# An encoder layer with neighbourhood attention on one Trainium2 core: TensorE in a written order, scores directly behind the keys, the values' projection among the score steps

## The chip, the cores and the metric

The kernel runs on one core of one Trainium2 chip. The metric is the device time of one execution in microseconds (us). The kernel before takes 1509.41 us (median of 3 runs, 1507.68 to 1510.08).

## The reference

One layer of an encoder on 1024 real tokens behind 16 meta tokens, model width 1024, float32. An RMSNorm, one combined input projection, a branch of neighbourhood attention (8 heads of width 64) and a branch with a gated linear recurrence, both gated and joined, an output projection, and a feed-forward part. The change lies in the attention branch and in the projections of its queries, keys and values:

```python
a = rms_norm(h, norm_mix[l])
(q_na, k_na, v_na, ...) = split_cols(a @ w_in[l])
...
def neighbourhood_attention(q, k, v, rpb):
    # a real token sees an 8 x 16 window of the 64-wide grid, and all 16 meta keys
    s_win = einsum('brchd,bjrwhd->...', qg, k_blk) * dh ** -0.5
    s_win = where(in_win, s_win + bias, -1e30)
    s = concatenate([s_win, s_meta], axis=-1)
    p = softmax(s, axis=-1)
    o_grid = einsum(p_win, v_blk) + einsum(p_meta, vm)
```

## The kernel before, in words

Matrix products are made in three passes with operands that are split into a high and a low part (`mm3`, L122 to L124: high times high, high times low, low times high). The weights come in blocks of 128 columns: `load_block` loads a block over SP's queue (`raw`, L102), ScalarE writes its high part `hi` (L112, or L115 with a factor for the queries), VectorE its low part `lo` (L113 or L116). Each of `raw`, `hi` and `lo` has two buffers. The block after next therefore gets its `hi` and `lo` only when the projection that used the same buffer has ended. `proj_steps` starts that split (`early[nxt]`) at the start of a projection.

The attention works on four pairs of heads (`for p in range(NPAIR)`). For each pair it projects the queries (`ev_q`), the keys (`ev_k`, with the meta keys in `mev_k`) and the values (`ev_vn`). Each projection is three pieces of 24 matmuls for the keys and values (256, 272 and 512 columns) or two pieces for the queries (512 each), into PSUM tiles `mm` out of three banks. The last piece of the keys leaves PSUM like this: ScalarE copies the high part of head 0 and of head 1 into `KS` (L802), VectorE writes the low parts into `KL` (L805), ScalarE copies `KS` onto the other half of the partitions (L807). A strip holds 8 columns of all 16 grid rows, so every strip needs the last piece.

Then come 16 steps, one for each strip `s` of 8 and each head `i` of 2. `scores` makes two matmuls into `nsc` (L848 with `KS`, L849 with `KL`; two banks), VectorE subtracts the mask and finds the extreme (L854), ScalarE takes the exponential (L856), VectorE scales by the reciprocal of the sum (L857, L858). `values` turns the weights (L869, L871: transposes on TensorE into `ppt`, tag "t", two banks), ScalarE and VectorE split them into `PT` (L880, L881), and after every fourth step it makes the products with the values into `pov` (L885 to L894), which leave over `low` (L896, VectorE) and `OT` (L898). The values themselves are turned once a pair (L831 into `vpt`, on the same two banks as `ppt`) and split into `Vn` (L833, L834). At most three steps are open (`pend`).

What sets the order: in the written part (`in_order`, up to the keys of pair 0) the engines run what the code says. After that a scheduler puts each engine's instructions in a row when the program is built. It is the scheduler that moves projections of the next pair, or the first gate products behind pair 3 (L928 to L930), between the score steps. The rows are fixed then: at run time each engine takes its row in order and waits at a semaphore where an operand is not there.

Of the kernel before, what the change touches and what calls it, by code (L numbers as in the profile page):

```python
# [9 lines left out]
F32 = mybir.dt.float32  # L10
# [3 lines left out]
ALU = mybir.AluOpType  # L14
# [4 lines left out]
P = 128  # L19
D = 1024  # L20
KC = D // P
T = 1024
TH = 512
# [3 lines left out]
NPAIR = 4  # L27
# [4 lines left out]
C_QN, C_KN, C_VN, C_Q, C_ZF, C_ZB, C_I, C_G, C_GN, C_GH = (  # L32
    0, 512, 1024, 1536, 2048, 2560, 3072, 3584, 4096, 5120)
# [15 lines left out]
def layer(ctx: ExitStack, tc: tile.TileContext, x, meta, w_in, w_na, w_hg, w_o, w_up, w_dn,  # L49
# [23 lines left out]
    def bank(tag, name):  # L73
        return banks[tag].tile([P, 4, P], F32, tag=tag, name=name)
# [58 lines left out]
    def proj(*args, **kw):  # L133
        for _ in proj_steps(*args, **kw):
            pass
# [15 lines left out]
    def block_of(col):  # L151
        return early.pop(col, None) or load_block(w_in[:, col:col + P], KC, -0.125 if C_QN <= col < C_KN else None)
# [551 lines left out]
    early = {}  # L704
# [27 lines left out]
        next(cur)  # L732
        prev = cur

    def first_query():

        hi, lo = block_of(C_QN)
        early[C_KN] = block_of(C_KN)
        for h in range(2):
            ps = bank("mm", "mm").rearrange("p a b -> p (a b)")  # L740
            for k in range(KC):
                mm3(ps, hi[:, k], lo[:, k], *(t[:, k, :TH] for t in aT[h]), k == 0, k == KC - 1)
            yield ps

    in_order = ExitStack()
    in_order.enter_context(tc.manual_schedule(engines={e.engine for e in (pe, act, dve)}))
    query_ps = list(first_query())
    list(prev)
    hps.close()

# [6 lines left out]
    with (tc.tile_pool(name="npr", bufs=1, side="right", reuse_waits="tile") as npr,  # L757
# [10 lines left out]
        def strips(t, p0, t0, n, w=None):  # L768

            a = t[p0:p0 + 64, 0:8, t0 // 8:(t0 + n) // 8]  # L770
            return a.rearrange("p s (r c) -> p s r c", c=8)

        def grid(ps, p0):
            return ps[p0:p0 + 64].rearrange("p (r s c) -> p s r c", s=8, c=8)

        for p in range(NPAIR):
            NB = npl.tile([P, 2, 1024], F32, tag="NB", name="NB")
            for i in range(2):
# [8 lines left out]
            def ev_q(ps, t0, n):  # L787
                for i in range(2):
                    act.copy(strips(QX[i], 64 * i, t0, n), grid(ps, 64 * i))
                for i in range(2):  # L790
                    b = 64 * i
                    dve.tensor_tensor(strips(QX[i], 64 - b, t0, n), grid(ps, b),
                                      strips(QX[i], b, t0, n).bitcast(F32), op=ALU.subtract)
            if p == 0:
                for h in range(2):
                    ev_q(query_ps[h], h * TH, TH)
            else:
                proj(C_QN + p * P, ev_q)

            def ev_k(ps, t0, n):  # L800
                for i in range(2):
# [7 lines left out]
            def mev_k(ps):  # L809
                for i in range(2):  # L810
# [12 lines left out]

            def mev_vn(ps):
                act.copy(vT[:, 8, P - NM:], ps)
            proj(C_VN + p * P, ev_vn, mev_vn)
            for b in (0, 4, 8):
                pt = bank("t", "vpt")
                m = min(4, 9 - b)
                for j in range(m):  # L830
                    pe.transpose(pt[:, j], vT[:, b + j], ident)  # L831
                src = pt[:, :m].rearrange("p j (i d) -> p j i d", i=2)
                act.copy(V[:, b:b + m, :, :64], src)  # L833
                dve.tensor_tensor(V[:, b:b + m, :, 64:], src, V[:, b:b + m, :, :64].bitcast(F32), op=ALU.subtract)  # L834

            block_sums(p, lambda: npl.tile([P, TH], F32, tag="bs", name="rt", bufs=3))

            po = {}
# [22 lines left out]
            def values(s, i, js, pr):  # L861
# [16 lines left out]
                for k, n, b in runs:  # L878
                    hi = PH[:, b:b + 3 * n - 2:3]
                    act.copy(hi, pt[:, k:k + n])  # L880
                    dve.tensor_tensor(PL[:, b:b + 3 * n - 2:3], pt[:, k:k + n], hi.bitcast(F32), op=ALU.subtract)  # L881
                if e < 3:
                    return
                ov = bank("b", "pov")
                pe.matmul(ov, V[:, 8, i], PH[:, 9:22:4], start=True, stop=False)  # L885
                for a in range(-1, 5):
# [6 lines left out]
                        pe.matmul(ov[:64, e0:e0 + ne], V[:, j, i, :64], PL[:, b:b + ne], start=False, stop=False)  # L893
                pe.matmul(ov, V[:, 8, i], PL[:, 9:22:4], start=False, stop=True)  # L894
                low = npr.tile([64, 4, P], F32, tag="low", name="low")
                dve.tensor_copy(low, ov[64:])  # L896
# [5 lines left out]
            pend = []  # L902
# [880 lines left out]
    with tc.manual_schedule(engines={sp.engine, dve.engine, act.engine, pool.engine}):  # L1783
# [5 lines left out]
        for n, (p_, m) in enumerate(steps):  # L1789
# [101 lines left out]
```

## Time and profile before

| | |
|---|---|
| median of 3 runs | 1509.41 us |
| the profiled execution's own time | 1509.18 us |
| its span in the profile | 1507.4 us |
| TensorE (PE) busy | 1491.1 us, 99% |
| VectorE (DVE) busy | 1045.3 us, 69% |
| ScalarE (ACT) busy | 670.0 us, 44% |
| GpSimd (POOL) busy | 363.2 us, 24% |

The profile gives for each instruction its start and duration on its engine, which tile it writes and reads, and what it waited for. A matmul's duration covers its way through the array, so successive matmuls overlap. The pace of TensorE is read from the distance of two starts. "PEld" is the load of the weights into the array, which runs ahead of the matmul. L12 is line 12 of the kernel.

### The profile page before, as it was taken

To read this page: it belongs to the slowest core of one execution; us is meant where nothing else is said; L and a number is where in the kernel's file an instruction comes from. 1 tells how busy PE (TensorE), PEld (TensorE's weight loads), DVE (VectorE), ACT (ScalarE), POOL (GpSimd) and SP (SyncE) were. 2 spreads that over 40 slices of the span, in tenths; PEclk is the share of its full clock that TensorE was granted. 3 is DMA by queue.
4 is the path that set the end of the run, shared out by engine and by line. 5 is a ranking of instruction groups with operands and counts; after the bars stand their busy time and mean duration, and the time that the engine had idled before them with its cause. 6 is when DMAs were issued, how large, how long until landed. Compare 5 with 4: busy or idle time off the path is not lost.

```text
span 1507.4 us, 23483 instructions
## 1 busy us (share of the span) xinstructions
PE 1491.1 (99%) x9200; PEld 1249.7 (83%) x9200; DVE 1045.3 (69%) x1612; ACT 670.0 (44%) x1197; POOL 363.2 (24%) x346
## 2 busy tenths in 40 slices
PE   9999999999999999999999999999999999999998
PEld 8888888888888888888888887888888888888886
DVE  7777767756786786675475479777777445877876
ACT  7131313135565576334233345555555534334444
POOL 3313131324414400110000121244444200231142
PEclk9999999999999999999999999999999999999999
DMA  4211111114222227444656124444444576563224
GB/s 170 59 29 57 29 56 31 44 31 131 85 65 95 98 85 264 140 148 169 223 160 223 42 96 164 167 154 154 154 154 154 202 255 233 190 229 114 96 84 154
DMA packets 142592, 195.61 MB, mean 130 GB/s; under 512 B 8193, under 2 KB 90369, under 8 KB 142481
## 3 DMA queue, kind: packets, MB, share of 16 engines
q1 hardware_dynamic: 133216, 172.86, 34.8%
q10 hardware_dynamic: 7088, 13.91, 2.4%
q0 software_dynamic: 2176, 7.34, 1.3%
q8 instruction: 72, 1.18, 0.3%
q14 instruction: 40, 0.32, 0.1%
HBM read 139.56 MB, written 54.53 MB: 129 GB/s over the span
## 4 chain that ended last, share of the span: by engine, by line
PE 87%; DVE 6%; DMA 2%; ACT 2%; issue 1%; POOL 1%; SPq 0%; ACTq 0%; POOLq 0%; DVEq 0%
PE mm L122 9%; PE mm L124 9%; PE mm L123 9%; PE mm L1564 5%; PE pa L1564 5%; PE pb L928 4%; PE pb L929 4%; PE pb L930 4%; PE pc L1564 4%; PE pb L1564 4%; PE pc L929 3%; PE pc L930 3%; PE pc L928 3%; PE pa L929 2%; PE pa L930 2%; PE pa L928 2%
## 5 line engine op out<-in xcount | busy, mean ns | idle before, releaser
L122 PE MATMUL mm<-aT,hi 128*128 128x512 f32 (+2 forms) x600 | 215.2, 359 | 0.0
L124 PE MATMUL mm<-aT,lo 128*128 128x512 f32 (+2 forms) x600 | 212.2, 354 | 0.0
L123 PE MATMUL mm<-aT,hi 128*128 128x512 f32 (+2 forms) x600 | 211.6, 353 | 0.0
L97 DVE TENSOR_TENSOR dl<-ur,dh 128x1024 fp32r<-128x1024 f32 x54 | 71.1, 1316 | 87.3 <-ACT dh L96 87.1
L96 ACT CAST dh<-ur 128x1024 fp32r<-128x1024 f32 x54 | 56.9, 1054 | 166.7 <-issue 91.1
L122 PEld LDWEIGHTS mm<-aT,hi 128*128 128x128 f32 x600 | 113.7, 190 | 12.6
L124 PEld LDWEIGHTS mm<-aT,lo 128*128 128x128 f32 x600 | 113.5, 189 | 12.8
L123 PEld LDWEIGHTS mm<-aT,hi 128*128 128x128 f32 x600 | 113.7, 190 | 11.6
L1352 ACT ACTIVATE uv<-uv 128x512 f32<-128x512 f32 x48 | 30.4, 633 | 79.3 <-DVE uv L1460 52.8
L112 ACT CAST hi<-raw 128x1024 fp32r<-128x1024 f32 x26 | 27.3, 1050 | 68.4 <-PE mm L123 65.4
L854 DVE CUSTOM_DVE_ANT_0 pr<-nsc,NB 128x432 f32<-128x432 f32 (+1 forms) x64 | 35.2, 559 | 29.7 <-issue 29.5
L1655 POOL TENSOR_TENSOR w<-w,tt 128x512 f32<-128x512 f32 x16 | 23.4, 1461 | 133.1 <-DVE tt L1654 112.3
L303 POOL TENSOR_TENSOR Y<-X,TN 128x512 f32<-128x512 f32 x20 | 31.6, 1578 | 85.1 <-DVE X L300 85.1
L113 DVE TENSOR_TENSOR lo<-raw,hi 128x1024 fp32r<-128x1024 f32 x26 | 39.5, 1520 | 15.8 <-ACT hi L112 11.8
L124 PE MATMUL mm<-wh,mT 128*128 128x512 f32 x128 | 50.0, 391 | 0.4 <-DVE mT L97 0.4
L122 PE MATMUL mm<-wh,mT 128*128 128x512 f32 x128 | 50.3, 393 | 0.0
L123 PE MATMUL mm<-wl,mT 128*128 128x512 f32 x128 | 50.1, 391 | 0.0
L124 PE MATMUL mm<-o,lo 128*128 128x512 f32 x128 | 49.9, 390 | 0.1
L123 PE MATMUL mm<-o,hi 128*128 128x512 f32 x128 | 49.8, 389 | 0.0
L122 PE MATMUL mm<-o,hi 128*128 128x512 f32 x128 | 49.8, 389 | 0.0
L1564 PE MATMUL mm<-dl,dh 128*128 128x512 f32 x124 | 48.6, 392 | 0.3 <-DVE dl L97 0.2
L1564 PE MATMUL mm<-dh,dl 128*128 128x512 f32 x124 | 48.3, 389 | 0.0
(459 smaller groups left out, 4434.8 us busy)
## 6 DMA issues: line engine op xcount, KB each, us to landing
raw<-in_w_in SPq DMA_DIRECT2D x56, 512.0 KB, 4.0
ur<-usp SPq DMA_DIRECT2D x54, 512.0 KB, 3.5
raw<-in_w_up SPq DMA_DIRECT2D x16, 1024.0 KB, 6.2
usp<-us SPq DMA_DIRECT2D x60, 256.0 KB, 2.3
sg<-gsp SPq DMA_DIRECT2D x16, 512.0 KB, 5.1
w<-in_w_dn SPq DMA_DIRECT2D x16, 512.0 KB, 4.6
usp<-uv SPq DMA_DIRECT2D x30, 256.0 KB, 2.3
gsp<-gv ACTq DMA_DIRECT2D x24, 256.0 KB, 2.4
```

The source lines that it names most:

```text
L96: act.copy(hi, src)
L97: dve.tensor_tensor(lo, src, hi.bitcast(F32), op=ALU.subtract)
L113: dve.tensor_tensor(lo[:, :kc], raw[:, :kc], hi[:, :kc].bitcast(F32), op=ALU.subtract)
L122: pe.matmul(ps, lh, rh, start=first, stop=False)
L123: pe.matmul(ps, lh, rl, start=False, stop=False)
L124: pe.matmul(ps, ll, rh, start=False, stop=last)
L303: pool.tensor_tensor(fap(Y, h, mid3), fap(X, h, mid3), fap(TT, 0, [[4, g], [n + 3, 2], [0, h]]), op=ALU.mult)
L854: dve.tensor_tensor_reduce(out=pr[:, :w], in0=sc[:, :w], in1=NB[:, i, o:o + w], scale=1.0, scalar=3.0e38, op0=ALU.add, op1=ALU.min, accum_ ...
L928: pe.matmul(ps, lhs[0][:, c], rhs[0][:, k], start=first and k == 0, stop=False, skip_group_check=True)
L929: pe.matmul(ps, lhs[0][:, c], rhs[1][:, k], start=False, stop=False, skip_group_check=True)
L930: pe.matmul(ps, lhs[1][:, c], rhs[0][:, k], start=False, stop=k == 3, skip_group_check=True)
L1564: pe.matmul(ps, a[n == 2][:, q, j * P:(j + 1) * P], b[n == 1][:, q], start=first and n == 0, stop=last and n == 2, skip_group_check=True)
```

## The change

The four projections and the 16 steps of each pair stay as they are, number and shape of all matmuls too. What changes is their order, which is now written out for TensorE (`manual_schedule` for `pe.engine`), up to step 6 of pair 3. After that the scheduler orders TensorE again, and VectorE and ScalarE are ordered by it throughout, behind the keys of pair 0.

- The scores of a pair stand directly behind the last piece of its keys.
- The values' projection, the turning of the values and the next pair's queries (`fills`) are the filler between the score steps. A table `GAPS` says how many columns of it go into each step.
- The weights of a step are turned three steps later instead of two (`len(pend) > 3`), and the products stand apart from `values`, one step on.
- The last three turnings of a pair and its last products (`tail`) go between the matmuls of the next pair's keys.
- `low` is copied by ScalarE (`act.copy`, L924) and no longer by VectorE.

```diff
+        def ev_q(h, i):
+            b = 64 * i
+            ps = query_ps[h]
+            act.copy(strips(QX[i], b, h * TH, TH), grid(ps, b))
+            dve.tensor_tensor(strips(QX[i], 64 - b, h * TH, TH), grid(ps, b),
+                              strips(QX[i], b, h * TH, TH).bitcast(F32), op=ALU.subtract)
+
+        def columns(fill, n):
+            ahead_by[0] -= n
+            while ahead_by[0] < 0:
+                ahead_by[0] += next(fill, -ahead_by[0])
+
+        GAPS = ([(830, 830)] * 5 + [(680, 680), (300, 600)]
+                + [(600, 0), (350, 350), (350, 350), (350, 600)] * 2 + [(600, 0)])
...
-            proj(C_KN + p * P, ev_k, mev_k)
+            fill = proj_steps(C_KN + p * P, ev_k, mev_k)
+            for f in tail:
+                columns(fill, 5 * 256)
+                f()
+            list(fill)
             in_order.close()
+            in_order.enter_context(tc.manual_schedule(engines={pe.engine}))
...
-            proj(C_VN + p * P, ev_vn, mev_vn)
-            for b in (0, 4, 8):
...
+            def fills():
+                yield from proj_steps(C_VN + p * P, ev_vn, mev_vn)
+                if p + 1 < NPAIR:
+                    queries = query_steps(p + 1, mm_tile)
+                    for _ in range(2):
+                        yield next(queries)
+                for b in (0, 4, 8):
...
+                if p + 1 < NPAIR:
+                    yield from queries
...
-                dve.tensor_copy(low, ov[64:])
+                act.copy(low, ov[64:])
...
-            for st in steps:
+            fill = fills()
+            pend, due, tail = [], [], []
+            for n, st in enumerate(steps):
                 pend.append((*st, *scores(*st)))
-                if len(pend) > 2:
-                    values(*pend.pop(0))
-            for st in pend:
-                values(*st)
-            pool.dma_start(osp[1][p], OT)
+                if n >= 12 and query_ps and not taken:
+                    ev_q(0, 0)
+                    taken.append((0, 0))
+                if p == NPAIR - 1 and n == 6:
+                    in_order.close()
+                    list(fill)
+                columns(fill, GAPS[n][0])
+                while due:
+                    products(*due.pop())
+                if len(pend) > 3:
+                    s, i, *q = pend.pop(0)
+                    values(s, i, *q)
+                    if s % 4 == 3:
+                        due.append((s, i))
+                columns(fill, GAPS[n][1])
+            list(fill)
```

Three places in the rows of the two built programs matter below. First TensorE at the end of the keys of pair 0 (`mm_4171` is their last piece), in the kernel before; `mm_4209` is the first piece of the values:

```order
L122 MATMUL mm_4171<-aT10_89,hi_3949 128x512
L123 MATMUL mm_4171<-aT11_90,hi_3949 128x512
L124 MATMUL mm_4171<-aT10_89,lo_3950 128x512
L122 MATMUL mm_4209<-aT00_87,hi_4099 128x256
L123 MATMUL mm_4209<-aT01_88,hi_4099 128x256
L124 MATMUL mm_4209<-aT00_87,lo_4100 128x256
```

The same place in the changed kernel, where `mm_4239` is the first piece of the values:

```order
L122 MATMUL mm_4171<-aT10_89,hi_3949 128x512
L123 MATMUL mm_4171<-aT11_90,hi_3949 128x512
L124 MATMUL mm_4171<-aT10_89,lo_3950 128x512
L874 MATMUL nsc_4222<-KS0_4067,QX0_4065 128x288
L875 MATMUL nsc_4222<-KL0_4069,QX0_4065 128x288
L122 MATMUL mm_4239<-aT00_87,hi_4099 128x256
L123 MATMUL mm_4239<-aT01_88,hi_4099 128x256
L124 MATMUL mm_4239<-aT00_87,lo_4100 128x256
```

Between the last keys and the first scores there stood 72 matmuls of the values' projection; now nothing stands there. Pairs 1 to 3 read the same.

Second, VectorE at that place in the kernel before (`lo_4206` is the low part of the next pair's query weights, `pr_4329` the first step's scores):

```order
L116 SCALAR_TENSOR_TENSOR lo_4206<-raw_4203,hi_4205 128x1024
L805 TENSOR_TENSOR KL0_4069<-mm_4171,KS0_4067 64x8x64
L805 TENSOR_TENSOR KL1_4070<-mm_4171,KS1_4068 64x8x64
L854 ISA pr_4329,mn_4330<-nsc_4326,NB_4076 128x288
L854 ISA mn_4330 128x1
```

and in the changed kernel:

```order
L116 SCALAR_TENSOR_TENSOR lo_4236<-raw_4233,hi_4235 128x1024
L813 TENSOR_TENSOR KL0_4069<-mm_4171,KS0_4067 64x8x64
L813 TENSOR_TENSOR KL1_4070<-mm_4171,KS1_4068 64x8x64
L880 ISA pr_4225,mn_4226<-nsc_4222,NB_4076 128x288
L880 ISA mn_4226 128x1
```

Nothing moved here: the split of the next weights still stands ahead of the keys' low part. On ScalarE the high part of the same weights (L115) stands ahead of the copies into `KS`, before and now, and in pair 3 the first gate weights (L96, L97) stand there.

Third, TensorE where the values of pair 0 are turned, in the kernel before (`mm_4706` is the next pair's queries, `vpt` the turned values):

```order
L124 MATMUL mm_4706<-aT00_87,lo_4206 128x512
L831 MATMUL vpt_4291<-ident_77,vT_4071 128x128 x4
L831 MATMUL vpt_4298<-ident_77,vT_4071 128x128 x4
L122 MATMUL mm_4706<-aT00_87,hi_4205 128x512
L848 MATMUL nsc_4385<-KS1_4068,QX1_4066 128x288
```

and in the changed kernel, with `ppt` the turned weights of step 2 (counted from 0):

```order
L895 MATMUL ppt_4404<-ident_77,pr_4296 128x128 x3
L897 MATMUL ppt_4404<-ident_77,pr_4296 128x128
L854 MATMUL vpt_4411<-ident_77,vT_4071 128x128 x4
L854 MATMUL vpt_4418<-ident_77,vT_4071 128x128 x4
L874 MATMUL nsc_4425<-KS1_4068,QX1_4066 128x432
L875 MATMUL nsc_4425<-KL1_4070,QX1_4066 128x432
L854 MATMUL vpt_4436<-ident_77,vT_4071 128x128
L122 MATMUL mm_4397<-aT00_87,hi_4235 128x512
```

The values are now turned behind the weights of step 2, where they were turned ahead of the first weights of the pair. All of these tiles take turns on the two banks of tag "t".

More of the change, by code (lines that the diff above doesn't have):

```diff
@@ L733, in layer, with query_steps @@
         prev = cur
-    def first_query():
-        hi, lo = block_of(C_QN)
-        early[C_KN] = block_of(C_KN)
+    query_ps = []
+    def query_steps(p, tile):
+        hi, lo = block_of(C_QN + p * P)
+        early[C_KN + p * P] = block_of(C_KN + p * P)
         for h in range(2):
-            ps = bank("mm", "mm").rearrange("p a b -> p (a b)")
+            ps = tile()
             for k in range(KC):
                 mm3(ps, hi[:, k], lo[:, k], *(t[:, k, :TH] for t in aT[h]), k == 0, k == KC - 1)
-            yield ps
+                if k == KC - 1:
+                    query_ps.append(ps)
+                yield TH
     in_order = ExitStack()
     in_order.enter_context(tc.manual_schedule(engines={e.engine for e in (pe, act, dve)}))
-    query_ps = list(first_query())
+    list(query_steps(0, lambda: bank("mm", "mm").rearrange("p a b -> p (a b)")))
     list(prev)
@@ L785, in layer @@
                                        op=ALU.subtract)
[L787 to L798, printed above, removed]
             def ev_k(ps, t0, n):
@@ L816, in mev_k @@
                     dve.tensor_tensor(KL[i][b:b + 64, :, P:], m, hi.bitcast(F32), op=ALU.subtract)
-            proj(C_KN + p * P, ev_k, mev_k)
+            for q in ((0, 0), (0, 1), (1, 0), (1, 1)):
+                if q not in taken:
+                    ev_q(*q)
+            query_ps.clear()
+            taken.clear()
+            fill = proj_steps(C_KN + p * P, ev_k, mev_k)
[3 more added lines that the diff above has]
+            list(fill)
             in_order.close()
+            in_order.enter_context(tc.manual_schedule(engines={pe.engine}))
             def ev_vn(ps, t0, n):
@@ L825, in mev_vn @@
                 act.copy(vT[:, 8, P - NM:], ps)
-            proj(C_VN + p * P, ev_vn, mev_vn)
-            for b in (0, 4, 8):
[L828 to L834, printed above, removed]
+            def fills():
[5 more added lines that the diff above has]
+                for b in (0, 4, 8):
+                    pt = bank("t", "vpt")
+                    m = min(4, 9 - b)
+                    for j in range(m):
+                        pe.transpose(pt[:, j], vT[:, b + j], ident)
+                    src = pt[:, :m].rearrange("p j (i d) -> p j i d", i=2)
+                    act.copy(V[:, b:b + m, :, :64], src)
+                    dve.tensor_tensor(V[:, b:b + m, :, 64:], src, V[:, b:b + m, :, :64].bitcast(F32), op=ALU.subtract)
+                    yield m * P // 3
+                if p + 1 < NPAIR:
+                    yield from queries
             block_sums(p, lambda: npl.tile([P, TH], F32, tag="bs", name="rt", bufs=3))
@@ L881, in values, with products @@
                     dve.tensor_tensor(PL[:, b:b + 3 * n - 2:3], pt[:, k:k + n], hi.bitcast(F32), op=ALU.subtract)
-                if e < 3:
-                    return
+            def products(s, i):
+                g = s // 4
+                PH, PL = po[i]
                 ov = bank("b", "pov")
@@ L901, in layer, with last @@
             steps = [(4 * g + e, i) for g in range(2) for i in range(2) for e in range(4)]
-            pend = []
-            for st in steps:
+            fill = fills()
+            pend, due, tail = [], [], []
+            for n, st in enumerate(steps):
                 pend.append((*st, *scores(*st)))
-                if len(pend) > 2:
-                    values(*pend.pop(0))
-            for st in pend:
-                values(*st)
-            pool.dma_start(osp[1][p], OT)
+                if n >= 12 and query_ps and not taken:
[14 more added lines that the diff above has]
+            list(fill)
+            def last(s, i, *q):
+                return lambda: values(s, i, *q)
+            tail += [last(*q) for q in pend]
+            tail += [lambda dst=osp[1][p]: (products(7, 1), pool.dma_start(dst, OT))]
+            if p == NPAIR - 1:
+                for f in tail:
+                    f()
     def winograd(eng, a11, a12, a21, a22, s1, s2, s3, s4):
```

2 lines of the change are left out of this document (added).

## The prediction

> **What bounds the kernel now.** I read the page first, then the stages, then the waits in the attention (330 to 565 us), then single stretches.
>
> ```profile
> span 1507.4 us, 23483 instructions
> PE 1491.1 (99%) x9200; PEld 1249.7 (83%) x9200; DVE 1045.3 (69%) x1612; ACT 670.0 (44%) x1197; POOL 363.2 (24%) x346
> ```
>
> The first row of the table by stage is the attention; its columns are length, then busy time of PE, PEld, DVE, ACT and POOL, and last the granted clock and the DMA's share:
>
> ```profile
> 330.00:565.00 235.00, 233.41 (x1412) 200.51 (x1411) 175.90 (x436) 146.57 (x342) 80.77 (x81) 1.00 0.28 90
> ```
>
> TensorE is busy for 99% of the span, and for 233.41 of the 235.00 us of the attention. It is idle there for 1.6 us by its modelled ends. VectorE has 59 us to spare there, ScalarE 88. So time can only come from TensorE: from waits that go, or from new ones. The number of its matmuls and their shapes stay, so nothing else is to be had.
>
> Who waited for whom in the same stretch (total us, times, longest):
>
> ```profile
> DVE pr L854 <- issue: 29.5, 4, 8.2
> PEld nsc L848 <- DVE mn L854: 5.3, 17, 0.6
> PEld ppt L869 <- issue: 4.0, 14, 0.5
> PEld pov L885 <- ACT PT L880: 1.7, 8, 0.2
> ```
>
> The first row is VectorE standing still four times, up to 8.2 us, while TensorE projects the values of a pair. That is what the new order fills, but VectorE is not the bound. The other three rows are the weight loads of scores, turnings and products, held up by 11.0 us in all. A load runs ahead of its matmul, so most of this passes while TensorE still works; 1.6 us is what shows as its idle time. The waits that the new order can remove are worth between 1.6 and 11.0 us.
>
> **The scores directly behind the keys: a new wait, four times.** The first scores need `KS` and `KL` of the last piece of the keys. What this takes shows at pair 0, where TensorE went on with the values' projection at 348.93:
>
> ```profile
> 348.93 0.28 PE L122 MATMUL mm<-aT,hi 128*128 128x256 f32 x1
> 348.90 1.06 ACT L115 ACTIVATE hi<-raw 128x1024 fp32r<-128x1024 f32 x1 [1.86 <-PE mm L123]
> 349.98 1.19 ACT L802 CAST KS<-mm 64x512 fp32r<-64x512 f32 x2
> 349.99 2.74 DVE L116 SCALAR_TENSOR_TENSOR lo<-raw,hi 128x1024 fp32r<-128x1024 f32 x1 [2.92 <-ACT hi L115]
> 351.07 1.26 ACT L807 CAST KS<-KS 64x512 fp32r<-64x512 f32 x2
> 352.76 1.39 DVE L805 TENSOR_TENSOR KL<-mm,KS 64x512 fp32r<-64x512 f32 x2
> ```
>
> The split of the next weights comes first on both engines, because its buffer falls free with the same last matmul: 1.06 us on ScalarE, then 2.74 us on VectorE. Only then does VectorE write `KL`; the row holds two instructions, so that of head 0 ends after half of 1.39 us, at 353.46. TensorE could have begun the second score matmul then, 4.53 us after the keys. It did not wait, since the values' projection covered this: in pair 1 from 406.31 to 417.67. The same stretch in pairs 1, 2 and 3:
>
> ```profile
> 406.31 0.28 PE L122 MATMUL mm<-aT,hi 128*128 128x256 f32 x1
> 407.38 1.23 DVE L116 SCALAR_TENSOR_TENSOR lo<-raw,hi 128x1024 fp32r<-128x1024 f32 x1 [2.79 <-ACT hi L115]
> 408.64 1.39 DVE L805 TENSOR_TENSOR KL<-mm,KS 64x512 fp32r<-64x512 f32 x2
> 417.67 0.29 PE L848 MATMUL nsc<-KS,QX 128*128 128x288 f32 x1
> ...
> 462.75 0.28 PE L122 MATMUL mm<-aT,hi 128*128 128x256 f32 x1
> 463.81 2.73 DVE L116 SCALAR_TENSOR_TENSOR lo<-raw,hi 128x1024 fp32r<-128x1024 f32 x1 [2.92 <-ACT hi L115]
> 466.57 1.39 DVE L805 TENSOR_TENSOR KL<-mm,KS 64x512 fp32r<-64x512 f32 x2
> ...
> 518.62 0.28 PE L122 MATMUL mm<-aT,hi 128*128 128x256 f32 x1
> 519.68 1.53 DVE L97 TENSOR_TENSOR lo<-raw,hi 128x1024 fp32r<-128x1024 f32 x1 [2.92 <-ACT hi L96]
> 521.24 1.39 DVE L805 TENSOR_TENSOR KL<-mm,KS 64x512 fp32r<-64x512 f32 x2
> ```
>
> By the same reading (start of `KL` plus 0.70, less the end of the keys) these are 3.03, 4.52 and 3.32 us. The rows of the changed program keep the split ahead of `KS` and `KL` in all four pairs, and nothing stands between the keys and the scores on TensorE, so the cover is gone and all of it becomes idle time of TensorE: 4.53 + 3.03 + 4.52 + 3.32 = 15.4 us. Behind the waiting matmul on TensorE stands the whole values' projection, which needs none of this. The ends: the split takes 1.23 us on VectorE at its best and 2.74 at its worst, so four times 3.0 to 4.5 us, 12.0 to 18.0 us. I take 15.4, the sum as it stands.
>
> **The clock behind a wait.** No wait of 3 us occurs in this trace's attention. The nearest row is the one place where the granted clock (next to last but one column) fell, and the stretch around 890 us for comparison:
>
> ```profile
> 59.68:63.09 3.41, 1.81 (x70) 0.99 (x68) 3.41 (x6) 0.37 (x1) 0.08 (x1) 1.00 0.28 83
> 63.09:66.51 3.42, 3.42 (x10) 2.76 (x11) 1.32 (x4) 0.52 (x2) 1.54 (x1) 0.50 0.00 0
> 889.11:892.53 3.42, 2.56 (x15) 1.90 (x14) 2.94 (x5) 2.15 (x5) 0.00 (x0) 1.00 0.02 6
> 892.53:895.94 3.41, 3.41 (x18) 2.88 (x17) 3.27 (x6) 2.86 (x6) 0.00 (x0) 1.00 0.67 200
> ```
>
> After 3.41 us with 1.6 us of idle time the next 3.42 us ran at half the clock; after 3.42 us with 0.86 us of it they did not. A matmul of 512 columns then starts every 0.42 us and no longer every 0.22:
>
> ```profile
> 64.18 0.63 PE L123 MATMUL mm<-aT,hi 128*128 128x512 f32 x1
> 64.60 0.63 PE L124 MATMUL mm<-aT,lo 128*128 128x512 f32 x1
> ...
> 67.09 0.39 PE L122 MATMUL mm<-aT,hi 128*128 128x512 f32 x1
> 67.31 0.39 PE L123 MATMUL mm<-aT,hi 128*128 128x512 f32 x1
> ```
>
> A wait of 3.0 to 4.5 us puts at least 1.5 us of idle time into one such stretch, however it falls. So I expect a slow stretch behind each of the four, worth half of 3.42, 1.7 us, less what of it TensorE still spends waiting, more where the wait reaches into two of them. I take 1.5 us each, 6.0 us. Ends: 0 if the clock holds, 2.9 us each (1.7 us, and half of what a second stretch has left, some 2.3 us) or 11.6 us.
>
> The Trainium skill, "TensorE: Matmul & The Clock Gate", section "Part 1: The HAM clock gate (the "warmup" mystery)", has the gate fall to half rate after an idle window of about 3.4 us that runs freely, and its closing table asks for no idle gaps over about 3 us. That speaks against this change. Read strictly, a whole idle window, it would spare the waits of 3.0 and 3.3 us and hit the two of 4.5 us at most, 3.4 us in place of 6.0 and a sum lower by 2.6 us. The trace fell after less than half a window of idle time and does not agree with the strict reading; I go by the trace.
>
> **Between the score steps.** The groups that matter, by line (busy us and mean ns of one behind the bar):
>
> ```profile
> L881 DVE TENSOR_TENSOR PT<-ppt,PT 128x512 fp32r<-128x512 f32 (+3 forms) x70 | 41.5, 598 | 0.9 <-ACT PT L880 0.3
> L880 ACT CAST PT<-ppt 128x512 fp32r<-128x512 f32 (+3 forms) x71 | 36.2, 514 | 20.8 <-PE ppt L871 18.8 <-DVE PT L881 1.4 <-PE pov L892 0.4
> L896 DVE COPY low<-pov 64x512 f32<-64x512 f32 x15 | 10.4, 692 | 1.7 <-PE pov L894 1.4
> L113 DVE TENSOR_TENSOR lo<-raw,hi 128x1024 fp32r<-128x1024 f32 x7 | 9.9, 1420 | 0.1
> L112 ACT CAST hi<-raw 128x1024 fp32r<-128x1024 f32 x7 | 7.4, 1054 | 13.3 <-PE mm L123 13.2
> ```
>
> Weights that are turned three steps later, with filler in each step, leave the chain of scores, exponential and scaling more time, so the three PEld rows above shrink. I take 4 us off, nearer to the 1.6 of the idle row than to the 11.0, because a PEld wait mostly lies beside running matmuls.
>
> Against it stands the turning of the values, now behind the weights of step 2, on the two banks that `ppt` uses. A bank comes back after a copy on ScalarE (0.51) and a subtraction on VectorE (0.60), 1.1 us, and the split of the next keys' weights (1.05 on ScalarE, then 1.42 on VectorE) starts just then, with the end of the values' projection. Four groups of transposes follow each other with only one pair of scores between them, so TensorE can wait for up to 2.5 us (1.1 and 1.4) in each of pairs 0 to 2, at least not at all. I take 1.0 us, about one bank's return: 3.0 us, from 0 to 7.5.
>
> Edits at nothing: `low` goes from VectorE (0.69 us, 16 times) to ScalarE, which has 88 us free; it would cost some 0.7 us a time only if products had to wait for `pov`, which is used every fourth step. The queries as filler and the tail among the next keys are the same matmuls elsewhere; their copies out of PSUM have a piece of the keys, 3 us or more, ahead of the next use of their bank. SP's and POOL's rows keep their order but for the store of `OT`, which is issued two places later at most and waits for nothing on the path.
>
> **The sum.** The profiled execution took 1509.18 us itself, 1.8 us more than its span and 0.2 under the median, 1509.41. 1509.2 + 15.4 + 6.0 + 3.0 - 4.0 = 1529.6 us.
>
> **The rivals.**
>
> *The clock holds.* The same waits, but no stretch at half rate, and the splits at their shorter durations: between 1509.2 + 12.0 + 3.0 - 4.0 = 1520.2 and 1523.6. For it speaks that the slow stretch in the trace also held small matmuls, which may count for less than a pause between dense ones; against it the two rows with 1.6 and 0.86 us. The skill's strict reading belongs here.
>
> *VectorE falls behind.* The splits are slow in every pair, the waits reach into two stretches, and the turning of the values costs its most: 1509.2 + 18.0 + 11.6 + 7.5 - 4.0 = 1542.3.
>
> *No change.* All 11.0 us of PEld waits were real and go, the four waits are 3.0 us each, the clock holds: 1509.2 - 11.0 + 12.0 = 1510.2.
>
> *Faster.* All 11.0 us go, at steps 4 to 15 of each pair, because VectorE no longer carries a backlog there (the 29.5 us it stood still are used), and the wait behind the keys is only the copy of head 0 and its `KL`, 0.6 + 0.7 = 1.3 us a pair: 1509.2 - 11.0 + 5.2 = 1503.4. It decides in favour of this below a mean wait of 2.75 us a pair. Against it: the split stands ahead of both in the built rows, and the shortest of the four stretches is 3.03 us.
>
> **How the numbers follow.** Forecast (1524 to 1537) 0.55, the clock holds 0.20, VectorE falls behind 0.15, no change 0.06, faster 0.04. The predicted time is that of the first, 1529.6. The range reaches from 1515 to 1540: below it takes in the held clock with a larger gain, above it most of the third case. A measurement here tells 0.2%, 3 us, from no change. Faster 0.04; of "no change" most lies within 3 us, 0.05; slower by over 0.2% is the rest, 0.91.
>
> **What would show it.** In the changed profile: TensorE idle for 3 to 4.5 us right behind each of the four last key pieces, released by `KL` or `KS`; the idle time of VectorE at L854's successor gone; the granted clock at 0.50 for about 3.4 us behind each; waits of `ppt` or `vpt` on VectorE near step 6; fewer PEld waits elsewhere. The prediction is wrong if TensorE's idle time behind the keys is under 2.75 us a pair, if the clock stays at 1.00 there, or if the rest of the steps gains more than 10 us.

## The result and the profile after

The changed kernel takes 1536.73 us (median of 4 runs, 1534.05 to 1537.77) against 1509.63 us (4 runs): a ratio of 1.018, 95% interval 1.0166 to 1.0195. The forecast was 1529.6 us, with a range up to 1540. The direction and the main mechanism came true; the size was 7.1 us short.

The page of the changed kernel, first and third line:

```profile
span 1535.1 us, 23461 instructions
...
PE 1496.8 (98%) x9200; PEld 1256.3 (82%) x9200; DVE 1041.4 (68%) x1596; ACT 682.4 (44%) x1213; POOL 361.7 (24%) x346
```

The same 9200 matmuls are 5.7 us longer busy in a span 27.7 us longer. To see where, I compare the stretch between the 3601st and the 5201st matmul, which holds the attention. First the kernel before, then the changed one (length, then busy time of PE, PEld, DVE, ACT, POOL, then clock and DMA):

```profile
325.49:598.28 272.79, 271.20 (x1602) 232.71 (x1601) 198.48 (x468) 167.83 (x376) 81.79 (x83) 1.00 0.34 111
```

```profile
324.00:626.94 302.94, 278.58 (x1602) 240.76 (x1601) 195.10 (x453) 180.06 (x392) 80.75 (x83) 0.97 0.31 100
```

The stretch grew by 30.15 us. TensorE's idle time in it went from 1.59 to 24.36 us, 22.8 more; its busy time grew by 7.4, at a clock that is no longer 1.00 throughout. (Ahead of the stretch the changed run is 1.5 us better, behind it 1.0: 27.7 in all.) TensorE's waits there, released by whom (total us, times, longest):

```profile
PE nsc L874 <- ACT KS L815: 10.6, 4, 2.6
PE vpt L854 <- DVE PT L907: 4.3, 3, 1.5
PE mm L973 <- ACT go L994: 3.0, 1, 3.0
PE nsc L875 <- DVE KL L813: 2.2, 4, 0.8
PE pov L913 <- ACT PT L906: 2.1, 3, 1.0
PE ppt L895 <- DVE Vn L857: 1.8, 3, 0.6
```

The first and fourth row are the waits behind the keys that the prediction spoke of, 12.8 us by the modelled ends of the matmuls. Counted from start to start, less the pace of a matmul, they are 3.9, 3.9, 3.4 and 3.3 us in the four pairs, 14.5 in all. The other waits are the turning of the values (4.3 and 1.8), the first gate product behind the attention (3.0) and the products (2.1). The keys of pair 0, on all engines; a bracket is the idle time ahead of the instruction and who ended it:

```profile
347.80 0.39 PE L124 MATMUL mm<-aT,lo 128*128 128x512 f32 x1
348.00 1.06 ACT L115 ACTIVATE hi<-raw 128x1024 fp32r<-128x1024 f32 x1 [1.28 <-PE mm L123]
349.08 1.19 ACT L810 CAST KS<-mm 64x512 fp32r<-64x512 f32 x2
349.09 2.12 DVE L116 SCALAR_TENSOR_TENSOR lo<-raw,hi 128x1024 fp32r<-128x1024 f32 x1 [2.34 <-ACT hi L115]
350.17 1.26 ACT L815 CAST KS<-KS 64x512 fp32r<-64x512 f32 x2
350.84 0.40 PE L874 MATMUL nsc<-KS,QX 128*128 128x288 f32 x1 [2.65 <-ACT KS L815]
351.25 1.41 DVE L813 TENSOR_TENSOR KL<-mm,KS 64x512 fp32r<-64x512 f32 x2
352.08 0.37 PE L875 MATMUL nsc<-KL,QX 128*128 128x288 f32 x1 [0.83 <-DVE KL L813]
```

On both engines the split of the next weights (L115, L116) stands ahead of the keys, as the built rows said. The first score starts 3.04 us after the last key matmul, the second another 1.24 later.

Now the clock. The rows are stretches of 3.41 us, cut where the clock may change; the last but two columns are the granted clock and the DMA's share:

```profile
349.53:352.94 3.41, 1.26 (x8) 1.08 (x9) 3.32 (x4) 3.13 (x5) 3.33 (x4) 1.00 0.19 77
352.94:356.36 3.42, 3.42 (x18) 3.42 (x18) 0.38 (x3) 0.63 (x2) 3.01 (x4) 0.50 0.02 5
...
410.97:414.38 3.41, 0.72 (x3) 0.19 (x1) 2.19 (x1) 3.20 (x5) 3.01 (x4) 1.00 0.50 143
414.38:417.79 3.41, 2.62 (x12) 2.62 (x13) 2.43 (x7) 0.78 (x3) 1.83 (x2) 0.50 0.31 85
417.79:421.20 3.41, 3.41 (x16) 3.35 (x16) 0.62 (x2) 0.17 (x1) 0.29 (x1) 0.50 0.66 215
...
479.23:482.64 3.41, 3.16 (x14) 3.16 (x15) 1.89 (x6) 0.78 (x3) 1.29 (x2) 0.50 0.41 92
...
537.26:540.67 3.41, 1.67 (x8) 1.05 (x6) 0.85 (x1) 1.88 (x3) 3.01 (x4) 1.00 0.38 154
540.67:544.08 3.41, 2.29 (x16) 2.08 (x17) 2.65 (x6) 2.09 (x5) 3.10 (x3) 1.00 0.36 98
...
598.70:602.11 3.41, 1.38 (x6) 1.16 (x7) 0.69 (x1) 2.98 (x5) 0.00 (x0) 1.00 1.11 384
602.11:605.52 3.41, 3.41 (x10) 2.64 (x9) 2.32 (x2) 1.96 (x4) 0.00 (x0) 0.50 0.82 317
```

The clock fell behind the keys of pairs 0, 1 (for two stretches) and 2, and behind the wait at the gate products. It did not fall in pair 3, where the same wait lies across the border at 540.67 and leaves 1.67 and 2.29 us of work on either side. Half of the busy time at half clock was lost: (3.42 + 2.62 + 3.41 + 3.16) / 2 = 6.3 us behind the keys, 3.41 / 2 = 1.7 behind the gate products, 8.0 in all.

### The profile page after: what moved, and what is told of

Its sections match the earlier page's. It is cut to its first block, busy times and chain, and to the rows that moved or that the text cites. A ratio compares the mean times of both kernels' runs of the same rounds, so it can differ in the third digit from the quotient of the medians.

```text
span 1535.1 us, 23461 instructions
## 1 busy us (share of the span) xinstructions
PE 1496.8 (98%) x9200; PEld 1256.3 (82%) x9200; DVE 1041.4 (68%) x1596; ACT 682.4 (44%) x1213; POOL 361.7 (24%) x346
## 3 DMA queue, kind: packets, MB, share of 16 engines
q8 instruction: 72, 1.18, 0.3%
## 4 chain that ended last, share of the span: by engine, by line
PE 60%; DVE 2%; ACT 1%; issue 1%; DMA 0%; POOL 0%; SPq 0%; ACTq 0%; POOLq 0%; DVEq 0%
PE mm L1609 5%; PE pa L1609 5%; PE pb L973 4%; PE pb L974 4%; PE pb L975 4%; PE pc L1609 4%; PE mm L124 4%; PE mm L122 4%; PE pb L1609 4%; PE mm L123 4%; PE pc L973 3%; PE pc L975 3%; PE pc L974 3%; PE pa L975 2%; PE pa L973 2%; PE pa L974 2%
## 5 line engine op out<-in xcount | busy, mean ns | idle before, releaser
L122 PE MATMUL mm<-aT,hi 128*128 128x512 f32 (+2 forms) x600 | 219.6, 366 | 0.3 <-DVE QX L784 0.3
L123 PE MATMUL mm<-aT,hi 128*128 128x512 f32 (+2 forms) x600 | 212.5, 354 | 0.0
L96 ACT CAST dh<-ur 128x1024 fp32r<-128x1024 f32 x54 | 56.9, 1054 | 166.7 <-issue 87.7
L97 DVE TENSOR_TENSOR dl<-ur,dh 128x1024 fp32r<-128x1024 f32 x54 | 71.1, 1316 | 87.4 <-ACT dh L96 87.1
L122 PEld LDWEIGHTS mm<-aT,hi 128*128 128x128 f32 x600 | 115.7, 193 | 11.8 <-PE mm L124 0.5
L123 PEld LDWEIGHTS mm<-aT,hi 128*128 128x128 f32 x600 | 115.9, 193 | 10.4
L882 ACT ACTIVATE pr<-pr,mn 128x432 f32<-128x432 f32 (+1 forms) x64 | 40.1, 627 | 43.1 <-DVE mn L880 42.5
L907 DVE TENSOR_TENSOR PT<-ppt,PT 128x512 fp32r<-128x512 f32 (+3 forms) x72 | 42.7, 596 | 8.7 <-ACT PT L906 8.5
```

The costliest lines, as they stand in the source:

```text
L96: act.copy(hi, src)
L97: dve.tensor_tensor(lo, src, hi.bitcast(F32), op=ALU.subtract)
L122: pe.matmul(ps, lh, rh, start=first, stop=False)
L123: pe.matmul(ps, lh, rl, start=False, stop=False)
L882: act.activation(pr[:, :w], pr[:, :w], AF.Exp, bias=mn, scale=-1.0, accum_out=sm)
```

## The experiments

My theory after the result: three things cost time, each a place where TensorE, in its written row, meets work of ScalarE and VectorE that is not ready. They are the keys (14.5 us and 6.3 of half clock), the turning of the values with the products behind it, and the first gate product behind the attention (4.7 us with its half clock). The rivals are in each expectation. The kernels ran in four groups, each against the kernel before on the same chip. The kernel before took 1508.3 to 1509.1 us there, against 1509.63 us beside the changed kernel, which was not run again in them. So what a kernel is said below to gain on the changed kernel by the medians can be too much by 0.5 to 1.4 us:

| kernel | median us | kernel before | ratio, 95% interval |
|---|---|---|---|
| `e1_split_behind` | 1532.34 | 1508.61 | 1.0150 (1.0132 to 1.0168) |
| `e2_values_between` | 1516.38 | 1508.61 | 1.0046 (1.0032 to 1.0060) |
| `e3_dummies` | 1533.24 | 1508.61 | 1.0162 (1.0141 to 1.0182) |
| `e4_turn_bank` | 1531.51 | 1508.61 | 1.0146 (1.0129 to 1.0163) |
| `e5_turn_spread` | 1511.87 | 1508.54 | 1.0022 (1.0012 to 1.0032) |
| `e6_products_later` | 1509.10 | 1508.54 | 1.0006 (0.9996 to 1.0015) |
| `e7_two_open` | 1518.09 | 1508.54 | 1.0062 (1.0046 to 1.0078) |
| `e8_low_back` | 1515.92 | 1508.54 | 1.0051 (1.0033 to 1.0069) |
| `e9_pair3_as_e5` | 1510.31 | 1509.14 | 1.0006 (0.9997 to 1.0015) |
| `e10_one_piece` | 1514.32 | 1509.14 | 1.0039 (1.0024 to 1.0054) |
| `e12_raw_pool` | 1508.32 | 1508.26 | 0.9999 (0.9990 to 1.0008) |
| `e13_after_raw_pool` | 1533.12 | 1508.26 | 1.0165 (1.0152 to 1.0179) |

**The split behind the keys** (`e1_split_behind`). ScalarE and VectorE are put in written order there, too, with the split of the next weights after the keys:

```diff
-            list(fill)
+            for _ in range(23 - kept[0]):
+                next(fill)
+            with tc.manual_schedule(engines={act.engine, dve.engine}) if p else ExitStack():
+                list(fill)
+                if p + 1 < NPAIR:
+                    early[C_QN + (p + 1) * P] = block_of(C_QN + (p + 1) * P)
```

(`kept` counts how many of the keys' 24 steps the tail has already taken.)

> The split of the next pair's query weights is made to stand behind the eviction of the last keys on ScalarE and VectorE in pairs 0 to 2; pair 3 is left as it is. My theory (the four waits behind the keys are the split's place in the two engines' rows): from the last key matmul ScalarE needs two copies and one half of the duplicate, 0.6 + 0.6 + 0.65, so the first score matmul comes 0.8 us sooner, and the second no longer waits for KL (1.1, 1.1 and 0.55 us now). 5.1 us go in waits. The idle time in a clock stretch falls to about 2 us, so some of the 6.3 us of half clock in pairs 0 to 2 go too: 1526 to 1532 us. Pair 3 keeps its wait of 3.3 us. Rival (the wait is the copies' own time, the split only fills it): no more than 1 us goes, 1536 us.

It took 4.4 us less than the changed kernel (6.5 between the profiled executions), by the median just above what I expected. Its keys of pair 0:

```profile
348.08 0.39 PE L124 MATMUL mm<-aT,lo 128*128 128x512 f32 x1
348.51 1.18 ACT L815 CAST KS<-mm 64x512 fp32r<-64x512 f32 x2 [1.50 <-PE mm L124]
350.39 0.40 PE L885 MATMUL nsc<-KS,QX 128*128 128x288 f32 x1 [1.92 <-ACT KS L820]
350.62 0.31 PE L886 MATMUL nsc<-KL,QX 128*128 128x288 f32 x1
```

The first score comes 2.31 us after the last key matmul in place of 3.04, and the second no longer waits. So the split's place is about half of each wait in pairs 0 and 1 and less in pair 2 (3.4 us before). The rest, 2 us, is the keys' own copies in the order in which they stand: the copy of head 1 out of PSUM (half of the 1.18 us) comes ahead of the copy of head 0 onto the other half of the partitions, for which the first score waits. What the other order would give was not run. The clock gave less back than expected:

```profile
468.04:471.45 3.41, 1.50 (x11) 1.07 (x10) 1.58 (x3) 2.76 (x5) 3.09 (x3) 1.00 0.49 135
471.45:474.86 3.41, 3.41 (x17) 3.37 (x16) 1.93 (x5) 1.21 (x3) 0.61 (x2) 0.50 0.40 135
529.48:532.89 3.41, 0.77 (x5) 0.31 (x3) 1.82 (x2) 2.82 (x5) 3.01 (x4) 1.00 0.19 77
532.89:536.30 3.41, 3.37 (x14) 3.05 (x15) 2.19 (x6) 1.15 (x3) 2.13 (x3) 0.50 0.70 217
```

Pairs 0 and 1 kept the clock. Pair 2 lost it although its wait is now 2.1 us, and pair 3, which was not touched, lost it because its wait now lies within one stretch.

**Cover behind the keys** (`e2_values_between`):

```diff
-        GAPS = ([(830, 830)] * 5 + [(680, 680), (300, 600)]
+        GAPS = ([(410, 410)] * 5 + [(680, 680), (300, 600)]
...
+            columns(fill, 4224)
             for n, st in enumerate(steps):
```

> The first two pieces of the values' projection (48 of 72 matmuls, 5.8 us) go back between the last keys and the first scores in all four pairs, and the first five steps get half the filler; all else is as in the changed kernel. My theory (missing cover behind the keys, with the clock drops that follow): 14.5 us of waits and 6.3 us of half clock go, the turning of the values and the gate products keep theirs: 1536.7 - 20.8 = 1516 us. Rival (the first steps need the filler more than the keys do: a step costs VectorE 1.9 us and TensorE then has only 1.9 us of work in it): up to 5 steps by 0.5 us in four pairs come back, 1526 us.

1516.4 us, as the theory had it. All four waits behind the keys and every half clock in the attention are gone. What is left of TensorE's waits:

```profile
PE vpt L854 <- DVE PT L907: 4.6, 3, 1.7
PE pov L913 <- ACT PT L906: 2.5, 3, 1.0
PE ppt L895 <- DVE Vn L857: 1.2, 2, 0.6
```

(1.5 us more stand in two smaller rows.) That the time is just the expected one is in part chance: the wait at the gate products went as well, with its half clock 4.7 us, which this edit does not touch (the last kernels come back to it), and against it turning and products cost 1.6 us more than in the changed kernel (9.8 against 8.2). The two profiled executions differ by 23.2 us (1536.87 and 1513.63): in the stretch TensorE's idle time fell by 14.2 us, from 24.36 to 10.16, and its busy time by 9.0, from 278.58 to 269.57, of which 8.0 are the half clocks. The medians differ by 20.4 us only. The profiled execution is the shortest of the six, with a mean granted clock of 0.999; the other five have 0.996 to 0.998, and one half clock lowers the mean of an execution by 0.001 (half of 3.41 us in 1512). So half clocks probably fell in them that this profile does not show. Of the rival's 10 us nothing is seen in the profile.

**The clock alone** (`e3_dummies`):

```diff
+            for q in range(2):
+                wt = bank("t", "wt")
+                for j in range(12):
+                    pe.transpose(wt[:, j % 4], ident, ident)
             for n, st in enumerate(steps):
```

> 24 useless transposes of the identity (110 ns each, 2.6 us) into the two free banks of tag t between the last keys and the first scores of each pair, 8 us of the time in which TensorE waits anyway; the result is unused. My theory (the half clock comes from idle time of the array in a stretch of 3.41 us): the waits stay as they are, the drops at 353, 414 to 421 and 479 go, 6.3 us: 1530 to 1531 us. Rival (it comes from something else than idle time, the traffic or the phase of the work): 1536 to 1538 us.

In pairs 1 to 3 the dummies lie in the wait, and the score starts as late as ever, 3.04 us after the last key:

```profile
412.64 0.39 PE L124 MATMUL mm<-aT,lo 128*128 128x512 f32 x1
412.87 2.78 PE L935 MATMUL wt<-ident 128*128 128x128 f32 x24
415.68 0.40 PE L874 MATMUL nsc<-KS,QX 128*128 128x288 f32 x1
```

The stretch behind the one with the dummies, by the table of stretches:

```profile
416.25:419.67 3.42, 2.77 (x21) 2.77 (x22) 2.29 (x6) 0.65 (x3) 1.68 (x2) 1.00 0.32 86
```

The clock stays at 1.00 there, where the changed kernel ran two stretches at 0.50. In pair 0 the built row has the dummies at 339.36 to 341.9, among the first keys and not behind the last. There they cost 2.6 us of working time, and the drop stayed (at 354.81, for 3.41 us): a control that was not planned. Pair 2 kept the clock, too. In pairs 1 and 2 the edit so gained (2.62 + 3.41 + 3.16) / 2 = 4.6 us of half clock. At the gate products, which it was not aimed at, the wait fell from 3.0 to 2.0 us, in two parts, and no half clock followed it: 2.7 us more. Less the 2.6 us of pair 0 these make 4.7, where the profiled executions differ by 4.1 us and the medians by 3.5. With the wait unchanged and the array at work, the clock holds: the drop comes from the idle array, and its price is apart from that of the wait.

**The turning** (`e4_turn_bank`):

```diff
-                    pt = bank("t", "vpt")
+                    pt = bank("t" if b == 4 else "b", "vpt")
```

> Of the three groups of turned values the first and the third go into the bank of tag b (free there), only the second into tag t. My theory (TensorE waits 1.66 and 0.76 us a pair in pairs 0 to 2 because four groups of transposes follow each other on two banks): 4 to 5.5 of the 7.3 us go: 1531 to 1533 us. Rival (it is ScalarE's and VectorE's time for splitting these groups, and the wait only moves on to the next turned weights): 1536 us.

1531.5 us, within the expectation, but for other reasons than I gave. Where the changed kernel stood, at the second group on tag t (time and engine, with VectorE's row at that place):

```profile
369.22 0.49 PE L895 MATMUL ppt<-ident,pr 128*128 128x128 f32 x3
369.66 0.60 PE L854 MATMUL vpt<-ident,vT 128*128 128x128 f32 x4
371.70 0.66 PE L854 MATMUL vpt<-ident,vT 128*128 128x128 f32 x4 [1.44 <-DVE PT L907]
...
368.68 1.22 DVE L113 TENSOR_TENSOR lo<-raw,hi 128x1024 fp32r<-128x1024 f32 x1
370.95 0.69 DVE L907 TENSOR_TENSOR PT<-ppt,PT 128x512 fp32r<-128x512 f32 x1
```

In the new kernel the wait moved to the third group, on tag b, whose bank the first still held:

```profile
PE vpt L854 <- DVE Vn L857: 3.7, 3, 1.3
```

So 6.1 us (4.3 and 1.8) became 3.7. The rest of the gain is the wait at the gate products, which was absent here too (4.7 us with its half clock), less a drop in pair 3 (at 540.21, 1.7 us), where the wait behind the keys now lay within one stretch.

**Turnings apart, products later** (`e5_turn_spread` and `e6_products_later`, on top of the second kernel):

```diff
                 for b in (0, 4, 8):
-                    pt = bank("t", "vpt")
+                    if p + 1 < NPAIR and b:
+                        yield next(queries)
+                    pt = bank("t" if b else "b", "vpt")
```

and in the second of them also

```diff
-                + [(600, 0), (350, 350), (350, 350), (350, 600)] * 2 + [(600, 0)])
+                + [(1100, 0), (100, 350), (350, 350), (350, 600)]
+                + [(600, 0), (350, 350), (350, 350), (350, 600), (600, 0)])
...
-                while due:
+                while due and n < 15:
...
+            tail += [lambda q=due.pop(): products(*q)]
```

> On top of the kernel with two pieces of the values between keys and scores (1516.4 us): the first group of turned values goes into the bank of tag b, and a step of the queries (three matmuls, 0.68 us) stands between the groups. My theory (too few banks for groups that follow each other): of the 8.7 us that TensorE waits at the turning in pairs 0 to 2 there (3.8, 2.9 and 2.9 in its trace, with some background) 6 to 7 go: 1509.5 to 1511 us. Rival (the backlog of ScalarE and VectorE at this place, whatever the banks): under 2 us go, 1515 us.

> The same, and two more changes of the order on TensorE: the products after step 15 stand in the next pair's keys with the rest of the tail, and the first products of a pair stand two query steps (1.4 us) later. My theory: the waits of products for the weights of their last step (1.2, 1.2 and 0.5 us) go too, so that what is left is what the written order gains between the steps, some 4 to 5 us against the kernel before: 1505 to 1508 us, faster than it. Rival (the gain between the steps was only the mirror of the waits elsewhere): no faster than the kernel before, 1509 to 1511 us.

1511.9 us and 1509.1: 4.5 us went with the turnings apart (I expected 5.4 to 6.9), 2.8 more with the products later. Together they are level with the kernel before, not faster: the 1505 to 1508 us that I expected did not come, and the rival's range holds. In the second of the two 2.4 us of TensorE's waits are left at the turning and the products, in seven waits of at most 0.7 us. The one at the gate products is back (2.2 us), with a half clock behind it (574.94, 3.41 us).

**Two edits that I had put at nothing, or into the gain** (`e7_two_open` turns `len(pend) > 3` into `> 2`, `e8_low_back` turns `act.copy(low, ...)` into `dve.tensor_copy(low, ...)`, both on top of the second kernel):

> On top of the kernel with two pieces of the values between keys and scores (1516.4 us): weights are turned two steps later, as in the kernel before, not three. My prediction gave the third step and the filler a gain of 4 us together. If the third step carries most of it, waits of the turned weights on VectorE's scaling come back: 1518 to 1521 us. If the filler alone carries it: 1516 us, within 1 us.

> On top of the kernel with two pieces of the values between keys and scores (1516.4 us): the copy of low is back on VectorE. My prediction put this edit at nothing: 1515.5 to 1517.5 us. Rival (on ScalarE it stands ahead of the copies of the turned weights and makes the products wait; or VectorE is at its limit in the steps and gets slower with it): 2 us or more to either side.

`low` is at nothing: 1515.9 against 1516.4 us, from different groups of runs. Two open steps in place of three gave 1518.1, 1.7 us more; in its profile two half clocks appear (at 369.12 and 488.59) that the second kernel's profile has not, and the waits of TensorE come to about the same. So the third step is worth at most some 2 us here, and whether it is worth anything is not settled.

**The gate products.** First I took pair 3's products back to their place (`e9_pair3_as_e5`: `while due and (n < 15 or p == NPAIR - 1)`, and the copies of the queries grouped two by two). `e10_one_piece` is the same with `columns(fill, 2048)` and `(620, 620)`.

> The kernel with products later (1509.1 us), but in pair 3 the products after step 15 stand where they stood before that, and the queries' two copies go ahead of their two subtractions. My theory: there the first gate product waited 2.2 us for a sigmoid on ScalarE behind late loads, and a clock drop followed it (1.7 us); with the old order of pair 3 both go, and 0.5 us in pair 0: 1505 to 1507 us, 2 to 3 us faster than the kernel before. Rival (the wait is a matter of the end of the attention, wherever the products stand): 1508.5 to 1509.5 us.

> The same with one piece of the values' projection (24 matmuls, 2.9 us) between the last keys and the first scores, not two, and the third more of the filler in the steps. My theory (a wait is what the cover lacks): 3.9 us less 2.9 in pairs 0 and 1, 3.4 less 2.9 in pairs 2 and 3, so 3 us more than with two pieces, and no clock drop, because under 1.9 us of idle time lie in a stretch: 1508 to 1510 us. Rival (the waits come back in full, because VectorE and ScalarE are held up by the values' own eviction): over 1515 us.

Both missed. The first took 1510.3 us, more than either range; the wait stayed (2.5 us, with a half clock behind it), as the rival had it: the products' place is not its cause. In the second the waits behind the keys went but for 1.0 us in pair 0, less than I expected; yet the time was 1514.3, since the values' projection now ends a step later and the first products wait for it (1.8 us), and the rest of the 4 us I did not trace.

Then I looked at what the gate wait hangs on in the changed kernel:

```profile
581.09 7.64 SPq L1076 DMA_DIRECT2D raw<-in_w_in  x2
588.77 2.62 SPq L1055 DMA_DIRECT2D gv<-tsp_t  x4
...
598.15 0.62 ACT L96 CAST aT<-gv 128x512 fp32r<-128x512 f32 x1 [0.81 <-DMA gv<-tsp_t]
598.79 1.28 ACT L994 ACT_TABLE_LOAD   x1
600.08 0.60 ACT L994 ACTIVATE go<-mm 128x512 f32<-128x512 f32 x1
```

TensorE waits for the bank that the sigmoid `go` (600.08) empties. In ScalarE's row that stands behind four copies of `gv`, these behind their loads, and the loads stand on SP's queue behind two loads of `raw`, which wait for the buffer of a gate block whose low part VectorE writes late. The kernel before issued `gv` 6.5 us ahead of the last products (561.6 against 568.1), the changed one 0.2 ahead (588.8 against 589.0). In the kernel before:

```profile
561.62 2.13 SPq L1010 DMA_DIRECT2D gv<-tsp_t  x4
```

The profiles of the other kernels agree, and show why the wait went from some of them that left this place alone. Where `gv` is issued at least 2.5 us ahead of the last products (second, fourth, fifth, seventh and eighth kernel) the wait is absent or 0.4 us; where it is issued between 0.3 us ahead and 0.3 behind (first, third, sixth, ninth and tenth) it is 1.1 to 3.4 us.

So I let GpSimd's queue issue these `raw` loads, in the ninth kernel (`e9_pair3_as_e5`) and in the changed one:

```diff
     def gate_raws(m):
...
-            sp.dma_start(t, w_in[:, c:c + P].rearrange("(k p) c -> p k c", p=P))
+            pool.dma_start(t, w_in[:, c:c + P].rearrange("(k p) c -> p k c", p=P))
```

> The kernel with two pieces between keys and scores, turnings spread and products later (1510.3 us), in which the loads of the gate blocks' sums (raw, in gate_raws) are issued by GpSimd's queue and no longer by SP's, where they wait for a late split of gate weights and hold up the loads of gv behind them. My theory (this place in SP's row is the cause of the wait at the gate products): gv is issued some 8 us sooner, the sigmoid no longer stands behind ScalarE's copies of gv, and the wait (2.5 us) and the half clock behind it (1.7) go: 1505.5 to 1507.5 us, 1.5 to 3.5 us under the kernel before. Rival (ScalarE's own row and its table load set that wait, or GpSimd's queue is slow and something waits for raw in its place): 1509 to 1511 us.

> The changed kernel itself with that one edit. My theory: its wait at the first gate product behind the attention (3.1 us) and the half clock behind that (1.7 us) are the part of the loss that the prediction did not name: 1531.5 to 1533 us. Rival: 1536 to 1538 us, as the changed kernel.

On the changed kernel the theory held: 1533.1 us, 0.1 above the range that I expected, and wait and half clock are gone. By the medians this is 3.6 us less; with each kernel taken against the kernel before in its own group it is 2.2. Its loads and the sigmoid:

```profile
577.31 2.53 SPq L1055 DMA_DIRECT2D gv<-tsp_t  x4
...
592.86 2.18 ACT L96 CAST aT<-gv 128x512 fp32r<-128x512 f32 x4
595.06 1.28 ACT L994 ACT_TABLE_LOAD   x1
596.35 0.60 ACT L994 ACTIVATE go<-mm 128x512 f32<-128x512 f32 x1
```

`gv` is issued 11.5 us sooner, and the sigmoid comes before TensorE has run out of matmuls (597.4 in the changed kernel). In the other kernel the wait moved on to a later sigmoid (1.6 us at 586.19, again behind a copy of `gv` that waited for its load), without a half clock. That kernel takes 1508.3 us, level with the kernel before, and misses the 1505.5 to 1507.5 us that I expected. Its stretch from the 3601st to the 5201st matmul:

```profile
324.14:597.45 273.31, 269.20 (x1602) 234.21 (x1601) 192.43 (x454) 178.59 (x392) 87.81 (x90) 1.00 0.35 112
```

TensorE is busy 2.0 us less than before (269.20 against 271.20) and idle 2.5 us more (4.11 against 1.59). This is the best of the kernels in the written order that I tried; none beats the kernel before.

## Why the prediction was right or wrong

- **The waits behind the keys** (15.4 us) were right in place and cause, and the sum was near: 14.5 us from start to start, 12.8 by modelled ends. With their half clock they are 19 of the 27.7 us, and with cover they go. That the sum came so near is in part luck. For the four pairs it had 4.5, 3.0, 4.5 and 3.3 us, and 3.9, 3.9, 3.4 and 3.3 came. It went by `KL` alone, behind splits of 2.74, 1.23, 2.73 and 1.53 us on VectorE, which now took 2.12, 2.33, 1.78 and 1.72; and 10.6 of the 12.8 us were ended by ScalarE's copy of `KS`, 2.2 by `KL`. That all of it was the split's doing was too simple: without the split ahead, 2.31 of the 3.04 us to the first score remain.
- **The clock behind a wait** (6.0 us): the size was right, 6.3, by luck, for the rule was not. I took 1.5 us of idle time in a stretch as enough, so expected a drop in all four pairs. Pair 3 had 1.74 us (3.41 less 1.67) and kept its clock; pair 1 paid for two stretches. The strict reading of the Trainium skill ("TensorE: Matmul & The Clock Gate", section "Part 1: The HAM clock gate (the "warmup" mystery)"), a whole idle window, does not agree with the trace either: the clock fell behind stretches with 1.26 and 1.38 us of work in them. That the windows run freely does agree: the drops at 352.94, 414.38 and 479.23 lie 18 and 19 times 3.413 us apart, and in every other profile with more than one drop the distances are whole multiples of it, too.
- **The turning of the values** (3.0 us, up to 7.5) was named with the right cause, two banks and VectorE's split of weights at that place, and mis-sized: 6.1 us by the waits' rows. I counted one bank's return; VectorE's row had the split (1.22 us) and a scaling ahead of the subtraction, and the next turned weights waited again.
- **The removed waits** (-4.0 us): the idle time of before, 1.6 us, went, and busy time besides half clock fell by 0.6, so 2.2. In `e12_raw_pool`, the best of the written order, busy time is 2.0 us lower than before. The gain is there and is about half of what I took. The products' waits (2.1 us) are a cost that I had at nothing.
- **What no part named**: the wait at the first gate product, 3.0 us and 1.7 of half clock. The prediction saw that SP's row kept its order, and it did; but a row in the same order can be held up longer at one of its entries. This is the largest part of the miss: 3.1 at the turning, 4.7 here, 2.1 at the products, 1.8 at the gain, less 2.6 at the keys (by modelled ends) and 2.5 outside the stretch, with 0.3 more of half clock: 6.9 of the 7.3 us between the forecast's and the measured difference of the profiled executions (20.4 and 27.7). Of the 2.5 us outside, 1.5 lie ahead of 80 us, where of these two only the kernel before ran a stretch at half clock; the 1.0 arises at two places far behind the attention, near 795 and 890 us of the kernel before, and was not traced.
- **The rivals.** "The clock holds" fell with the changed kernel's own rows (0.50 behind three of the four waits). "VectorE falls behind" was nearer at the turning (7.5 against 6.1) and had too much of the rest. "No change" and "faster" needed all 11.0 us of the weight loads' waits; of these three rows 7.1 us are left in the changed kernel's attention. "Faster" needed under 2.75 us a pair behind the keys as well; the first kernel shows that 2 us a pair are to be had by order alone, and that still leaves 1532.3.

## What to carry to other kernels

When filler is moved from behind a stage into the steps after it, price what it covered there: here the matmuls moved from behind the keys had covered 19 us of waits and half clock, and the steps that got them gained 2. Work that was balanced by a scheduler has its slack in several places at once, so a written row for one engine needs the rows of the others at each hand-over, and at the end of the stage also what stands on the load queue behind a late buffer. Ask for every expected wait on TensorE whether it can leave a stretch of 3.4 us less than half full, because then it costs half a stretch more.

## What the runs showed of the hardware

- Whether a wait costs a half clock depends on where the free-running stretch cuts it. In the 14 profiles, from 20 to 1480 us, each of the 18 stretches at full clock with up to 1.55 us of busy TensorE was followed by half clock, and none with over 1.82 us was. Between them both occurred: full clock followed at 1.60, 1.67 and five more up to 1.79, half clock at 1.66 and at 1.81 (in two profiles), the stretch of small matmuls near 60 us that the prediction shows. The same wait in pair 3 cost nothing in the changed kernel (1.67) and 1.7 us in the first experiment (0.77), at an equal length.
- A slow stretch that is itself not full is followed by another: 2.62 of 3.41 us busy at 414.38, and half clock until 421.20; with 3.16 and 3.42 it ended after one.
